# First conditioning vectors on TensorE in four column quarters, x first in the queue, and the first three projections cut in two along K

## The chip, the cores and the metric

The kernel runs on one core of one Trainium2 chip. The metric is device time of one execution in microseconds (us). Three runs of the kernel before took 1870.29, 1872.89 and 1874.12 us; the median, 1872.89, is what the change is held against. The profile comes from a further execution, which took 1885.09 us.

The names used below: PE is TensorE (matrix products; "PEld" its weight loads), DVE is VectorE, ACT is ScalarE, POOL is GpSimd, SP is the engine whose queue issues nearly all DMAs.

## The reference

Two layers over x (512 tokens by 1024 features), conditioned by a vector c. Layer 0 runs a state-space mixer (SSD) and a dilated window attention side by side; layer 1 is a convolution module; each layer ends with a SwiGLU FFN. What matters here is how the first layer begins:

```python
cs = jax.nn.silu(c)
for i in range(DEPTH):
    mod = cs @ ada_w[i] + ada_b[i]                       # 1024 -> 6*1024
    sh1, sc1, g1, sh2, sc2, g2 = [m[:, None, :] for m in jnp.split(mod, N_MOD, axis=-1)]
    h = rms_norm(x, norm_mix_g[i]) * (1 + sc1) + sh1
    ...
    z, xbc, dt_raw, q, k, v = jnp.split(h @ w_in, HY_SPLITS, axis=-1)   # hybrid_mixer
    xbc = jax.nn.silu(causal_depthwise_conv(xbc, conv_w, conv_b))
    xs, bm, cm = jnp.split(xbc, (SSM_D_INNER, SSM_D_INNER + SSM_GROUPS * SSM_STATE), axis=-1)
    dt = jax.nn.softplus((dt_raw + dt_bias).astype(jnp.float32))
    y = ssd_chunked(xs, dt, A, bm, cm)
```

Before any product with `w_in` can start, h needs the row statistics of x, the scale sc1 and the shift sh1, and these two are a vector-matrix product with 8 MB of `ada_w`.

## The kernel before

Activations are held transposed: feature tiles of 128 partitions by 512 tokens, eight of them (`h[k]`, k = 0..7). An exact product in float32 is made of three fast ones: weight and activation are each split in a high part and a low remainder (`hi`, `lo`; `hh`, `hl`), and `products` adds hi·hh, lo·hh and hi·hl over the eight k into one PSUM bank (24 matmuls of 128x512 for 128 output features).

The conditioning vectors are made in pieces of 512 columns, called by their first 128-column block: slabs 8 and 12 hold the scale (features 0-511 and 512-1023), slabs 0 and 4 the shift. Each slab is two DMAs of 1 MB (`ada_load`, `adaw`). `ada_wide` works on DVE: `adaa` = sum over k of `adaw[k]` times the scalar `cs[k]`, eight DVE operations of 128x512 (L160, L162); then `ada_finish` turns the result with four PE transposes (`ada`, L153) and sums over the free axis (`mod`, L155), adds the bias (L156). From slab 8 and 12 comes the gain `g_mix0`.

x is loaded as four token blocks `xin`. ACT squares them with a running sum (L316), a short DVE chain makes the reciprocal root (`rsqrt`), ACT scales the blocks (`xn`, L320), PE turns them (`xnp`, L331), ACT multiplies by the gain (`n_g`, L338), adds the shift and rounds to the high part (`n_h`, L341), DVE makes the low part (`n_l`, L343). x itself is turned too (`xtp`) and kept as `xT` (copied by ACT, L346).

The weight slabs of the projections (`slab`) are loaded by SP, rounded by ACT (`_h`, L194), and the remainder is made by the engine given (`_l`, L195): POOL for the first four slabs (`SL`), DVE after. The order of the first projections is dt (`wdt`), B and C of group 0 (`wbc0`, banks `bc0_0` and `bc0_1`), then four tiles of x (`wx`), four of z (`wz`). Two PSUM banks of the tag `pj` take turns for them: a new product can start only when the bank before last has been read, by ACT and three convolution steps of DVE (`conv_tile`, L443, L446).

dt goes through a long chain of small DVE operations (L403 to L419), a cumulative sum on PE, and a round trip through DRAM (`a_dram`, back as `ar` and `ef`) before the chunk loop of group 0 (`ssm_group`) can run. While that loop runs, PE makes the products of group 1, and so on for four groups. POOL makes further conditioning vectors in between (`ada_pool`, `adap`).

The order of the instructions on each engine is set by the Tile framework's scheduler from the program order and its own costs; `tc.issue_after` holds instructions behind a named one (here all of `after_ada` behind the last `ada_w` load, the first products behind the last transposes of slab 4). Semaphores keep the data right, the order is fixed at build time.

Of the kernel before, what the change touches and what calls it, by code (L numbers as in the profile page):

```python
# [17 lines left out]
P = 128  # L18
T = 512
# [58 lines left out]
def trunk_kernel(ctx: ExitStack, tc, a, out, dbg=None):  # L78
# [54 lines left out]
    S.activation(cs, pc, AF.Silu)  # L133
    slabs = {8: ada_load(first, 0, 8, nc.sync, 6)}
    pa = rows([(r128(a["norm_mix_g"][0]), 8), (r128(a["norm_ffn_g"][0]), 8),
               (r128(a["ada_b"][0]), 48), (r128(a["hy_conv_b"][0]), 24), (r128(a["hy_ssm_norm_g"][0]), 16)], "pa")
    xin = [first.tile([P, D], F32, tag="xin", name=f"xin{b}", bufs=NB) for b in range(NB)]
    for b in range(NB):
        nc.sync.dma_start(xin[b], a["x"][0, b * P:(b + 1) * P, :])
# [18 lines left out]
    def ada_wide(pool, tag, l, j0, ws):  # L158
        acc = pool.tile([P, 512], F32, tag=tag, name=f"adaa{l}_{j0}")
        V.tensor_scalar(acc, ws[0][:, 0, :], cs[:, 0:1], None, op0=ALU.mult)  # L160
        for k in range(1, KT):
            V.scalar_tensor_tensor(acc, ws[k // 4][:, k % 4, :], cs[:, k:k + 1], acc, op0=ALU.mult, op1=ALU.add)  # L162
        return ada_finish(l, acc, j0, 4)

# [154 lines left out]
    for b in range(NB):  # L319
        S.mul(xn[b], xin[b], rs[:, b:b + 1])  # L320
    g_mix0 = const.tile([P, KT], F32, name="g_mix0")
    for j0 in (8, 12, 0, 4):
        last_ada = ada_wide(tmp, "st_sq", 0, j0, slabs[j0])
        if j0 >= 8:
            k = slice(j0 - 8, j0 - 4)
            V.scalar_tensor_tensor(g_mix0[:, k], mod[0][:, j0:j0 + 4], 1.0, nmg0[:, k], op0=ALU.add, op1=ALU.mult)

# [7 lines left out]
    h = []  # L335
    for k in range(KT):
        t = first.tile([P, T], F32, tag="xg", name=f"n0_g{k}", bufs=KT)
        S.mul(t, turned(xn, k, "A" if k % 2 else "B", "xnp"), g_mix0[:, k:k + 1])  # L338
        hh = hpool.tile([P, T], F32R, tag="hh", name=f"n0_h{k}")
        hl = hpool.tile([P, T], F32R, tag="hl", name=f"n0_l{k}")  # L340
        S.activation(hh, t, AF.Identity, bias=mod[0][:, k:k + 1])  # L341
        with tc.issue_after(last_ada.ins) if LATE else nullcontext():
            V.scalar_tensor_tensor(hl, t, mod[0][:, k:k + 1], hh.bitcast(F32), op0=ALU.add, op1=ALU.subtract)  # L343
        h.append((hh, hl))
    for k in range(KT):
        S.copy(xT[k], turned(xin, k, XTP[k % 2], "xtp"))  # L346
    ctx_f.close()

    if "h" in dbg:
        for k in range(KT):  # L350
            t = tmp.tile([P, T], F32, tag="st_sq", name=f"dbgh{k}")
            V.tensor_tensor(t, h[k][0].bitcast(F32), h[k][1].bitcast(F32), op=ALU.add)
            nc.sync.dma_start(dbg["h"][k * P:(k + 1) * P, :], t)


    win = a["hy_w_in"][0]
    after_ada = tc.issue_after(marks["ada"].ins) if AFT else nullcontext()
    after_ada.__enter__()
# [16 lines left out]
    nc.sync.dma_start(nega, a["hy_a_log"][0:1, :].broadcast_to([P, HEADS]))  # L375

# [7 lines left out]
    w = slab([(win[:, 5120:5248], KT, P)], "wdt", SL[0])  # L384
    after_ada.__exit__(None, None, None)
    with tc.issue_after(marks["adat"].ins) if GDT else nullcontext():
        (dps,) = products(w, [grid(P, 0)], h, "dt")
# [65 lines left out]
    def ssm_inputs(g):  # L453
        w = slab([(win[:, 4096 + g * P:4096 + (g + 1) * P], KT, P), (win[:, 4608 + g * P:4608 + (g + 1) * P], KT, P)],
                 f"wbc{g}", SL[1] if g == 0 else V)
        pb, pc = products(w, [grid(P, 0), lambda k: 1024 + k * P], h, f"bc{g}")
# [3 lines left out]
        for j in range(2):  # L460
            o = 2048 + g * 512 + j * 256
            w = slab([(win[:, o:o + 256], KT, 256)], f"wx{g}_{j}", SL[2 + j] if g == 0 else V)
# [630 lines left out]
```

## Time and profile before

| What | us |
|---|---|
| median of three runs | 1872.89 (1870.29 to 1874.12) |
| profiled execution, whole | 1885.09 |
| its span, first to last instruction | 1882.8 |
| PE busy in the span | 1774.7 (94%) |
| DVE / ACT / POOL busy | 1046.5 / 693.1 / 430.5 |
| chain of work that ended last: PE, DVE, DMA | 73%, 11%, 7% of the span |

The profiled execution is 12 us longer than the median, so differences are worked out inside the profile and then set against the median. PE counts as busy from a matmul's start to its modelled end; two fast matmuls of 128x512 in a row start 0.23 us apart at full clock although each is recorded with 0.39 us. A float32 matmul appears as two records.

### The profile page before, as it was taken

The page shows a single profiled execution, that of the slowest core. Times are in us where ns is not written, and L with a number is a line of the kernel's source. Part 1 is how long each engine was busy: PE and PEld are TensorE (multiplying, and loading weights), DVE is VectorE, ACT ScalarE, POOL GpSimd, SP SyncE. Part 2 cuts the span into 40 slices and gives each one's busy share as a digit, 9 for nine tenths or more (in the row PEclk, how much of TensorE's full clock was granted, in tenths as well). Part 3 has the DMA queues.
Part 4 walks back from the last instruction along what each step waited for, and adds up shares of the span by engine and source line. Part 5 has one row for each costly group of instructions (what it writes and reads, how often), then busy time and mean ns, then how long its engine had stood idle before and what let it go on. Part 6 is the DMA issues. An engine that isn't in the chain of part 4 may idle for free.

```text
span 1882.8 us, 24868 instructions
## 1 busy us (share of the span) xinstructions
PE 1774.7 (94%) x9735; PEld 1450.0 (77%) x9735; DVE 1046.5 (56%) x1978; ACT 693.1 (37%) x1331; POOL 430.5 (23%) x328
## 2 busy tenths in 40 slices
PE   5897978999999999997999999999999999999998
PEld 3676766777778878777888888897567988888888
DVE  7858687755565565558665664373204743333336
ACT  6333333334545454344421221253214632122225
POOL 1437686422443440003000000013020200000001
PEclk8998989999999999997999999999998999999999
DMA  8354454545444443424555553253640523322223
GB/s 301 102 138 140 141 141 134 137 112 152 123 128 149 133 125 122 124 74 141 181 190 190 188 201 114 79 169 80 180 132 1 169 77 102 101 89 93 87 94 130
DMA packets 232066, 247.84 MB, mean 132 GB/s; under 512 B 13946, under 2 KB 198076, under 8 KB 231949
## 3 DMA queue, kind: packets, MB, share of 16 engines
q1 hardware_dynamic: 220813, 204.31, 36.6%
q0 software_dynamic: 11136, 41.95, 6.8%
q8 instruction: 77, 1.26, 0.3%
q14 instruction: 40, 0.33, 0.1%
HBM read 228.73 MB, written 8.64 MB: 126 GB/s over the span
## 4 chain that ended last, share of the span: by engine, by line
PE 73%; DVE 11%; DMA 7%; ACT 3%; issue 2%; POOL 2%; SPq 1%; DVEq 0%; ACTq 0%; POOLq 0%
PE fd L207 4%; PE fd L208 4%; PE fd L210 4%; PE fg L208 4%; PE fg L207 4%; PE fu L207 4%; PE fu L208 4%; PE fu L210 4%; PE fg L210 4%; PE cps L959 2%; PE s L717 2%; DMA ar<-a_dram 2%; PE wa L207 1%; PE wa L208 1%; PE wa L210 1%
## 5 line engine op out<-in xcount | busy, mean ns | idle before, releaser
L249 POOL TENSOR_TENSOR n_acc<-n_acc,n_q 128x256 f32<-128x256 f32 x32 | 29.7, 929 | 561.8 <-ACT n_q L245 561.7
L207 PE MATMUL fd<-uh,wd_h 128*128 128x512 f32 (+1 forms) x448 | 148.6, 347 | 0.9 <-DVE xT L592 0.9
L195 DVE TENSOR_TENSOR wf_l<-wf_w,wf_h 128x1024 fp32r<-128x1024 f32 x88 | 106.1, 1241 | 74.4 <-ACT wf_h L194 74.4
L208 PE MATMUL fd<-uh,wd_l 128*128 128x512 f32 (+1 forms) x448 | 147.0, 344 | 0.0
L194 ACT CAST wf_h<-wf_w 128x1024 fp32r<-128x1024 f32 x88 | 87.7, 1048 | 115.7 <-PE fd L210 71.9
L208 PE MATMUL fg<-n_h,wf_l 128*128 128x512 f32 x320 | 126.1, 394 | 2.0 <-DVE wf_l L195 2.0
L207 PE MATMUL fg<-n_h,wf_h 128*128 128x512 f32 x320 | 126.3, 395 | 0.7 <-ACT wf_h L194 0.5
L208 PE MATMUL fu<-n_h,wf_l 128*128 128x512 f32 x320 | 124.7, 390 | 0.0
L207 PE MATMUL fu<-n_h,wf_h 128*128 128x512 f32 x320 | 124.6, 389 | 0.0
L172 POOL TENSOR_TENSOR adap<-adap 128x128 f32<-128x128 f32 (+2 forms) x96 | 103.5, 1082 | 4.7
L869 DVE TENSOR_TENSOR fs<-fs,fu 128x512 f32<-128x512 f32 x40 | 27.5, 688 | 130.2 <-PE fu L210 130.2
L743 ACT ACTIVATE s<-s,nm 128x128 f32<-128x128 f32 x192 | 79.4, 415 | 50.7 <-DVE nm L739 40.4
L194 ACT CAST wd_h<-wd_w 128x1024 fp32r<-128x1024 f32 (+1 forms) x64 | 57.1, 941 | 101.2 <-PE fd L210 80.6
L592 DVE SCALAR_TENSOR_TENSOR xT<-fd,mod,xT 128x512 f32<-128x512 f32 (+1 forms) x64 | 39.1, 615 | 98.1 <-PE fd L210 97.8
L207 PEld LDWEIGHTS fd<-uh,wd_h 128*128 128x128 f32 x448 | 84.1, 188 | 12.0 <-DVE xT L592 1.3
L208 PEld LDWEIGHTS fd<-uh,wd_l 128*128 128x128 f32 x448 | 84.2, 188 | 10.5
L210 PE MATMUL fd<-ul,wd_h 128*128 128x512 f32 (+1 forms) x448 | 91.9, 343 | 0.0
L170 POOL TENSOR_TENSOR adap<-adap,cs 128x1024 f32<-128x1024 f32 x32 | 67.6, 2112 | 90.3 <-DMA adap<-in_ada_w 90.2
L195 DVE TENSOR_TENSOR wd_l<-wd_w,wd_h 128x1024 fp32r<-128x1024 f32 (+1 forms) x64 | 67.7, 1090 | 34.7 <-ACT wd_h L194 34.4
L162 DVE SCALAR_TENSOR_TENSOR adaa<-adaw,cs,adaa 128x512 f32<-128x512 f32 x112 | 84.8, 758 | 2.6
L210 PEld LDWEIGHTS fd<-ul,wd_h 128*128 128x128 f32 x448 | 72.9, 188 | 10.6
L210 PE MATMUL fg<-n_l,wf_h 128*128 128x512 f32 x320 | 79.1, 389 | 0.0
(400 smaller groups left out, 4584.5 us busy)
## 6 DMA issues: line engine op xcount, KB each, us to landing
adaw<-in_ada_w POOLq DMA_DIRECT2D x24, 1024.0 KB, 5.7
wf_w<-in_ffn_w_gate SPq DMA_DIRECT2D x22, 1024.0 KB, 5.2
wf_w<-in_ffn_w_up SPq DMA_DIRECT2D x22, 1024.0 KB
adap<-in_ada_w POOLq DMA_DIRECT2D x32, 512.0 KB, 5.5
wd_w<-in_ffn_w_down SPq DMA_DIRECT2D x16, 1024.0 KB, 5.1
wd_w<-in_ffn_w_down SPq DMA_DIRECT2D x16, 768.0 KB, 4.6
wa_w<-in_hy_w_out SPq DMA_DIRECT2D x20, 512.0 KB, 4.1
u<-cu SPq DMA_DIRECT2D x128, 67.5 KB, 2.0
```

The source lines that it names most:

```text
L162: V.scalar_tensor_tensor(acc, ws[k // 4][:, k % 4, :], cs[:, k:k + 1], acc, op0=ALU.mult, op1=ALU.add)
L170: G.tensor_tensor(w3, w3, cs.unsqueeze(2).broadcast_to([P, KT, P]), op=ALU.mult)
L172: G.tensor_tensor(w[:, 0:n], w[:, 0:n], w[:, n:2 * n], op=ALU.add)
L194: S.copy(hi[:, s:e], raw[:, s:e])
L195: eng.tensor_tensor(lo[:, s:e], raw[:, s:e], hi[:, s:e].bitcast(F32), op=ALU.subtract)
L207: PE.matmul(ps[:, cols], hi[:, o(k):o(k) + P], xh, start=k == 0, stop=False)
L208: PE.matmul(ps[:, cols], lo[:, o(k):o(k) + P], xh, start=False, stop=False)
L210: PE.matmul(ps[:, cols], hi[:, o(k):o(k) + P], acts[k][1][:, cols], start=False, stop=k == nk - 1)
L592: V.scalar_tensor_tensor(xT[m][:, cols], ps[:, cols], mod[l][:, go + m:go + m + 1], xT[m][:, cols], op0=ALU.mult, op1=ALU.add)
L717: marks[hp, 0] = marks[hp, 1] = PE.matmul(ps[:, o:o + 2 * wd].rearrange("p (e w) -> p e w", e=2), q, k, start=True, stop=True)
L743: S.activation(s[:, o:o + wd], s[:, o:o + wd], AF.Exp, bias=nm, accum_out=l)
L959: PE.matmul(ps[g * 32:(g + 1) * 32, :], w4[k][:, g * 8 + m, :], u4[k][:, g, t:t + w], start=m == 0, stop=m == 7)
```

## The change

1. SP's queue: x (four blocks) is issued ahead of slab 8; after that come the dt weights, slab 0, the B and C weights, slab 12 and slab 4. The loads of `wx0_0` and `wx0_1` are held behind the last `ada_w` load.
2. The four vectors are made by `ada_rows` on PE: silu(c) lies in column 0 of a 32-column weight tile (`cs32`, the other 31 columns zero); for each k a float32 matmul of 128 rows by 32 columns with 512 moving columns goes to one quarter of the output partitions (quarter k mod 4), so a vector takes eight such matmuls (`adar`). DVE copies the bank (`adas`), four float32 matmuls with one column of ones add the partitions (`adac`), one DVE operation adds the bias. The 32 DVE operations of 128x512, the 16 transposes and the 4 reductions of before are gone.
3. Two of the four `xn` blocks are scaled by DVE instead of ACT, and `xT` is copied by DVE instead of ACT.
4. The remainders of `wdt`, `wbc0`, `wx0_0`, `wx0_1` are made by DVE instead of POOL.
5. h is made in two halves of features (k = 0..3, k = 4..7). The products of dt, B and C are made for the first half, then for the second (`first_products`), and a fixed order is written out between them: dt and B first half; slab 12; C first half; slab 4; dt, B and C second half. C takes a bank of tag A instead of `pj`.

```diff
+    xin = [...]                                   # now ahead of slab 8
+    for b in range(NB):
+        nc.sync.dma_start(xin[b], a["x"][0, b * P:(b + 1) * P, :])
+    cs32 = first.tile([P, KT, 32], F32, name="cs32", bufs=1)
+    V.memset(cs32, 0.0)
+    V.tensor_copy(cs32[:, :, 0], cs)
     slabs = {8: ada_load(first, 0, 8, nc.sync, 6)}
...
-    slabs[12] = ada_load(first, 0, 12, nc.sync, 6)
-    for j0 in (0, 4):
-        slabs[j0] = ada_load(first, 0, j0, nc.sync, 6)
...
+    def ada_rows(l, j0, ws):
+        ps = bank("C", f"adar{l}_{j0}")
+        for k in range(KT):
+            g = k % 4
+            PE.matmul(ps[g * 32:(g + 1) * 32, :], cs32[:, k, :], ws[k // 4][:, g, :], start=k < 4, stop=k >= 4)
+        rw = tmp.tile([P, 512], F32, tag="st_sq", name=f"adas{l}_{j0}")
+        V.tensor_copy(rw, ps)
+        pm = bank("C", f"adac{l}_{j0}", (P, 4))
+        for j in range(4):
+            marks['adac', j0] = PE.matmul(pm[:, j:j + 1], rw[:, j * P:(j + 1) * P], ones[:, 0:1], start=True, stop=True)
+        marks['mod', j0] = V.tensor_tensor(mod[l][:, j0:j0 + 4], pm, adab[l][:, j0:j0 + 4], op=ALU.add)
...
-        S.mul(xn[b], xin[b], rs[:, b:b + 1])
+        if b % 2:
+            marks['xn'] = V.tensor_scalar(xn[b], xin[b], rs[:, b:b + 1], None, op0=ALU.mult)
+        else:
+            S.mul(xn[b], xin[b], rs[:, b:b + 1])
...
-    for j0 in (8, 12, 0, 4):
-        last_ada = ada_wide(tmp, "st_sq", 0, j0, slabs[j0])
...
+    def first_gain(j0):
+        ada_rows(0, 8 + j0, slabs[8 + j0])
+        kk = slice(j0, j0 + 4)
+        V.scalar_tensor_tensor(g_mix0[:, kk], mod[0][:, 8 + j0:12 + j0], 1.0, nmg0[:, kk], op0=ALU.add, op1=ALU.mult)
+        for k in range(j0, j0 + 4):
+            t = ng[k] = first.tile([P, T], F32, tag="xg", name=f"n0_g{k}", bufs=6)
+            S.mul(t, turned(xn, k, "BABABABB"[k], "xnp"), g_mix0[:, k:k + 1])
+
+    def first_shift(j0):
+        ada_rows(0, j0, slabs[j0])
+        for k in range(j0, j0 + 4):
+            hh, hl = h[k]
+            S.activation(hh, ng[k], AF.Identity, bias=mod[0][:, k:k + 1])
+            V.scalar_tensor_tensor(hl, ng[k], mod[0][:, k:k + 1], hh.bitcast(F32), op0=ALU.add, op1=ALU.subtract)
...
+    first_gain(0)
+    wdt = slab([(win[:, 5120:5248], KT, P)], "wdt")
+    slabs[0] = ada_load(first, 0, 0, nc.sync, 6)
+    wbc0 = slab([(win[:, 4096:4096 + P], KT, P), (win[:, 4608:4608 + P], KT, P)], "wbc0")
...
+    for j0 in (12, 4):
+        slabs[j0] = ada_load(first, 0, j0, nc.sync, 6)
+    with after('xn'):
+        for k in range(KT):
+            V.tensor_copy(xT[k], turned(xin, k, XTP[k % 2], "xtp"))
+    first_shift(0)
+    pre = [(wdt, grid(P, 0), bank("pj", "dt_0")), (wbc0, grid(P, 0), bank("pj", "bc0_0")),
+           (wbc0, lambda k: 1024 + k * P, bank("A", "bc0_1"))]
+
+    def first_products(jobs, ks):
+        for (hi, lo), o, ps in jobs:
+            for k in ks:
+                PE.matmul(ps, hi[:, o(k):o(k) + P], h[k][0], start=k == 0, stop=False)
+                PE.matmul(ps, lo[:, o(k):o(k) + P], h[k][0], start=False, stop=False)
+            for k in ks:
+                marks['fp'] = PE.matmul(ps, hi[:, o(k):o(k) + P], h[k][1], start=False, stop=k == KT - 1)
+
+    first_products(pre[:2], range(0, 4))
+    with after('fp'):
+        first_gain(4)
+    with after(('adac', 12)):
+        first_products(pre[2:], range(0, 4))
+    with after('fp'):
+        first_shift(4)
+    with after(('adac', 4)):
+        first_products(pre, range(4, KT))
...
+            with after('ada') if g == 0 else nullcontext():
+                w = slab([(win[:, o:o + 256], KT, 256)], f"wx{g}_{j}")
```

Three places in the order of instructions matter below. Names carry the layer or group first and a buffer number last: `adar0_12` is layer 0, slab 12; `n0_h4` is the high part of feature tile 4.

On PE, between the first products and their end. Before, dt and B run through all eight feature tiles:

```order
L153 MATMUL ada0_4_209<-cst_72,adaa0_4_200 128x128 x4
L110 MATMUL cw_p_363<-cst_72,cw_r_361 128x96
L207 MATMUL dt_0_399<-n0_h0_231,wdt_h_393 128x512
L208 MATMUL dt_0_399<-n0_h0_231,wdt_l_394 128x512
L207 MATMUL dt_0_399<-n0_h1_242,wdt_h_393 128x512
L208 MATMUL dt_0_399<-n0_h1_242,wdt_l_394 128x512
```

Now, after the last first-half product of B:

```order
L407 MATMUL bc0_0_336<-n0_l3_156,wbc0_h_226 128x512
L170 MATMUL adar0_12_362<-adaw0_12_0_254,cs32_95 32x512 x4
L170 MATMUL adar0_12_362<-adaw0_12_1_256,cs32_95 32x512 x4
L341 MATMUL xnp4_381<-cst_72,xn0_114 128x128
...
L175 MATMUL adac0_12_373<-ones_74,adas0_12_371 128x1 x4
L404 MATMUL bc0_1_337<-n0_h0_149,wbc0_h_226 128x512
...
L170 MATMUL adar0_4_420<-adaw0_4_0_258,cs32_95 32x512 x4
L170 MATMUL adar0_4_420<-adaw0_4_1_260,cs32_95 32x512 x4
...
L175 MATMUL adac0_4_431<-ones_74,adas0_4_429 128x1 x4
L404 MATMUL dt_0_335<-n0_h4_157,wdt_h_213 128x512
```

Slab 12, sixteen transposes of `xn` and slab 4 now stand in PE's queue between the two halves of the products; before, all of them stood ahead of the first product.

On DVE, ahead of the first shift. Before, the low parts of h follow the last bias add at once:

```order
L113 COPY cw_365<-cw_p_363 128x96
L156 TENSOR_TENSOR mod0_121<-mod0_121,pa_99 128x4
L343 SCALAR_TENSOR_TENSOR n0_l0_232<-n0_g0_224,mod0_121,n0_h0_231 128x512
L343 SCALAR_TENSOR_TENSOR n0_l1_243<-n0_g1_235,mod0_121,n0_h1_242 128x512
L343 SCALAR_TENSOR_TENSOR n0_l2_254<-n0_g2_246,mod0_121,n0_h2_253 128x512
```

Now:

```order
L208 TENSOR_TENSOR wbc0_l_227<-wbc0_w_223,wbc0_h_226 128x1024
L378 TENSOR_SCALAR cwh_238<-cw_236 128x96
L208 TENSOR_TENSOR wbc0_l_227<-wbc0_w_223,wbc0_h_226 128x1024
L465 TENSOR_SCALAR nega_251<-nega_251 128x32
L172 COPY adas0_0_319<-adar0_0_310 128x512
L176 TENSOR_TENSOR mod0_112<-adac0_0_321,pa_110 128x4
L368 SCALAR_TENSOR_TENSOR n0_l0_150<-n0_g0_183,mod0_112,n0_h0_149 128x512
```

The copy that closes slab 0 stands behind the remainder of the B and C weights and behind `nega`, both of which wait for ACT.

On SP, the DRAM round trip of dt's cumulative sum. Before:

```order
L435 DMA a_dram_384<-arow_471 32x512
L186 DMA wbc1_w_1110<-in_hy_w_in 128x8x128 x2
L486 DMA ar0_0_844<-a_dram_384 128x8x128
L561 DMA b_dram_826<-bv_832 16x896
L486 DMA ar0_1_880<-a_dram_384 128x8x128
L186 DMA wx1_0_w_1185<-in_hy_w_in 128x8x256
L186 DMA wx1_1_w_1259<-in_hy_w_in 128x8x256
```

Now:

```order
L199 DMA wbc1_w_1117<-in_hy_w_in 128x8x128 x2
L199 DMA wx1_0_w_1192<-in_hy_w_in 128x8x256
L483 DMA a_dram_483<-arow_537 32x512
L199 DMA wx1_1_w_1266<-in_hy_w_in 128x8x256
L538 DMA ar0_0_851<-a_dram_483 128x8x128
L613 DMA b_dram_833<-bv_839 16x896
L565 DMA ef0_1_914<-a_dram_483 64x4x128 x2
L538 DMA ar0_1_887<-a_dram_483 128x8x128
```

The first read of `ar` moved behind both x weight loads of group 1, the second also behind the first `ef` loads.

More of the change, by code (lines that the diff above doesn't have):

```diff
@@ L334, in trunk_kernel @@
     xT = [const.tile([P, T], F32, name=f"xT{k}") for k in range(KT)]
[L335 to L353, printed above, removed]
+    h = [(hpool.tile([P, T], F32R, tag="hh", name=f"n0_h{k}"), hpool.tile([P, T], F32R, tag="hl", name=f"n0_l{k}"))
+         for k in range(KT)]
```

36 lines of the change are left out of this document (20 added, 16 removed).

## The prediction

> **What bounds the kernel now.** I read the stretches of the span first (columns: PE, PE weight loads, DVE, ACT, POOL busy us, then the granted TensorE clock, DMA share, GB/s), then the DMA rate in slices of 3.25 us from the start.
>
> ```profile
> 0.00:40.00 40.00, 17.71 (x86) 12.96 (x87) 28.93 (x60) 26.20 (x40) 4.27 (x7) 0.90 0.91 310
> 60.00:70.00 10.00, 4.80 (x20) 3.30 (x18) 9.96 (x8) 0.84 (x1) 10.00 (x7) 1.00 0.34 105
> 70.00:80.00 10.00, 7.52 (x28) 6.18 (x29) 8.07 (x14) 2.41 (x5) 3.14 (x4) 0.83 0.34 107
> 80.00:130.00 50.00, 49.32 (x250) 38.41 (x248) 28.31 (x38) 19.83 (x28) 10.22 (x6) 1.00 0.49 131
> 130.00:180.00 50.00, 38.38 (x186) 29.93 (x187) 44.73 (x54) 18.50 (x28) 35.18 (x23) 0.89 0.41 117
> 400.00:1882.00 1482.00, 1439.22 (x8098) 1188.07 (x8096) 751.60 (x1592) 540.59 (x1109) 221.03 (x177) 0.98 0.41 126
> ```
>
> ```profile
> GB/s 61 367 378 400 391 388 387 386 388 311 293 66 44 332 294 72 282 6 3 0 239 83 163 160 5 0 72 271 0 137 84 159 284 5 0 269 198 123 117 297
> ```
>
> From 400 us on PE is busy 97% of the time, so what the start wins or loses is carried to the end. PE stands idle 22.3 us in the first 40, 7.7 from 60 to 80, 11.6 from 130 to 180 (there DVE is busy 44.7 of 50). DMA runs at some 388 GB/s until 35.75 us: eleven slices, 12.2 MB, which is ada_w, x, and the dt, B and C weights.
>
> The chain of waits (start, us) and the rows in time order say what opens the products and what stalls later:
>
> ```profile
> 2.06 7.62 DMA adaw<-in_ada_w
> ...
> 36.08 1.67 DVE adaa L162
> 37.79 1.11 PE ada L153 x4
> ...
> 38.77 0.78 PE L207 MATMUL dt<-n_h,wdt_h 128*128 128x512 f32 x1
> ...
> 50.09 0.57 ACT L389 COPY draw<-dt 32x512 f32<-32x512 f32 x1 [6.21 <-PE dt L210]
> ...
> 56.16 1.98 PE L210 MATMUL bc<-n_l,wbc_h 128*128 128x512 f32 x8
> ...
> 64.46 0.50 PE L208 MATMUL x<-n_h,wx_l 128*128 128x512 f32 x1 [3.34 <-POOL wx_l L195]
> ...
> 72.48 0.47 PE L207 MATMUL x<-n_h,wx_h 128*128 128x512 f32 x1 [4.34 <-DVE sc L446]
> ...
> 80.29 0.78 ACT L443 ACTIVATE sx<-x,cbh,cwh 128x512 f32<-128x512 f32 x1 [0.48 <-PE x L210]
> ```
>
> The last slab's DVE sums end at 37.8; products start at 38.8; dt is read at 50.1; C ends at 58.1; the second x tile ends at 80.3, after stalls of 3.3 us (POOL late with a remainder) and 4.3 us (a bank not yet read).
>
> **The change part by part.**
>
> *Transfers.* Same bytes, other order. x takes slab 8's place and lands at 2.06 + 7.62 = 9.7 instead of 15.1 (last square below). At 2.7 us for 1.05 MB the rest lands: slab 8 at 15.1, dt weights 16.5, slab 0 21.9, B and C 24.6, slab 12 30, slab 4 35.6, x weights 38 and 41. SP's queue now holds slab 12 behind slab 0's landing, with 1 MB of B and C still queued (2.7 us): 0 to 1 us of gap, I take 0; nothing waits for it, since PE comes to slab 12 later.
>
> ```profile
> 15.14 1.06 ACT L316 ACTIVATE xn<-xin 128x1024 f32<-128x1024 f32 x1
> 16.33 0.17 DVE L317 TENSOR_SCALAR n_ss<-n_ss 128x4 f32<-128x4 f32 x1 [0.28 <-ACT xn L316]
> ...
> 20.62 0.15 DVE L226 SCALAR_TENSOR_TENSOR n_y<-n_t,n_y 128x4 f32<-128x4 f32 x1
> 21.10 4.27 ACT L320 ACTIVATE xn<-xin,n_y 128x1024 f32<-128x1024 f32 x4
> ...
> 116.71 1.09 PE L504 MATMUL pd<-ar,xdt 128*64 128x128 f32 x16
> 117.73 1.12 PE L526 MATMUL pst<-xde,btok 128*128 128x512 f32 x2
> 118.69 0.39 PE L497 MATMUL pb<-sc,sb 128*128 128x128 f32 x2
> 118.91 0.60 PE L492 MATMUL px<-cst,sx 128*128 128x128 f32 x4
> ```
>
> *Norm.* The squares end at 11.0. The DVE chain of 12 small steps takes 4.4 us between rows of `adaa`; free of them, at 0.2 us a step, 2.4: 13.4. Two blocks on ACT, two on DVE: `xn` ready at 15.5 instead of 25.4.
>
> *One vector on PE.* No row has quarter-width matmuls. A float32 128x512 starts its follower 0.96 us later (`pst`, 117.73 to 118.69). One after another, eight cost 7.7 us; four abreast, 1.9. The nearest row is `pd`: eight of half width, alternating halves, take 1.02 us, where eight of full width cost 8 x 0.22 (`pb` to `px`) = 1.76, so halves overlap to 0.58. Twice that step, 0.58 squared times 7.7, gives 2.6; I take 2.4, near the abreast end because of `pd`. The Trainium skill, "TensorEngine Tiling (Array Packing)", Tiling Modes, has 128x32 as four independent tiles but says that a change of tiling mode drains the array; by its full fourfold the vector would cost 1.9 and the sum below gain 1.5 us more. The `pd` row agrees in kind; no run here shows quarters.
>
> ```profile
> 14.96 0.69 DVE L155 TENSOR_REDUCE mod<-ada 128x4 f32<-128x512 f32 x1 [1.21 <-PE ada L153]
> ...
> 26.21 4.74 ACT L338 ACTIVATE n_g<-xnp,g_mix 128x512 f32<-128x512 f32 x8
> 26.96 2.39 PE L331 MATMUL xnp<-cst,xn 128*128 128x128 f32 x16 [0.89 <-ACT n_g L338]
> 30.97 1.28 ACT L416 ACT_TABLE_LOAD   x1
> 32.77 2.56 ACT L341 ACTIVATE n_h<-n_g,mod 128x512 fp32r<-128x512 f32 x4
> 36.27 2.17 ACT L194 CAST wbc_h<-wbc_w 128x1024 fp32r<-128x1024 f32 x2
> ...
> 95.43 1.20 DVE L195 TENSOR_TENSOR wz_l<-wz_w,wz_h 128x1024 fp32r<-128x1024 f32 x1
> ```
>
> *First products.* Slab 8 on PE from 17 (behind eight transposes and `pa`), partly at half clock, 3 us; copy 0.7 (as L155's read of a bank), column sums 0.6, two adds: gain at 24. ACT: four `n_g` at 0.59 to 26.5, B and C casts 2.17, table load and `nega` 1.5: 30.3. On DVE the copy for slab 0 stands behind the B and C remainders (2 x 1.2) and `nega`: 30.5 to 31.2, though slab 0 itself left PE before 30. Sums, bias, first `n_h` 0.64: first product at 33.1, 5.7 earlier. The eight `xT` copies, 0.7 each, lie on DVE before that, beside the wait for slab 8.
>
> *To the end of C.* PE now has in its queue: 72 products at 0.227 ((1.98 - 0.39)/7) = 16.3; slabs 12 and 4, 4.8; 16 transposes, 2.4; eight column sums, 1.2; waits for copy, bias and `n_h` after each slab, 2.4. Together 27.1: C ends at 60.2, 2 us later than before, and dt with it, 10 us later. The early start is eaten by what moved between the halves.
>
> *The x tiles.* Their high parts queue on ACT behind the read of dt (60 to 62), the remainders on DVE, not on a busy POOL: tile 0 runs 62 to 67.5. Tile 1 waits for B's bank: four remainders (4.8) and five convolution steps (0.67 each) on DVE from 61.4 to 70, plus 2 for POOL's `adap`, which still runs then. It ends at 78, 2 us ahead of before: from C's end to there two tiles of 5.45 us lose 7 us now, 11.3 before (22.2 less 10.9), where the two stalls were followed by a stretch at half clock (0.83 in the row from 70).
>
> ```profile
> 52.49 0.29 DVE L403 TENSOR_TENSOR dt_v<-dt_t,dtb 128x128 f32<-128x128 f32 x1 [0.90 <-PE dt_t L392]
> 56.72 2.36 DVE L410 TENSOR_TENSOR dt_w<-dt_w 128x128 f32<-128x128 f32 x1
> 74.45 0.29 DVE L419 TENSOR_TENSOR dta<-dt_v,nega 128x128 f32<-128x128 f32 x1
> 98.91 0.36 SPq L486 DMA_DIRECT2D ar<-a_dram  x1
> 105.30 1.90 POOL L487 TENSOR_TENSOR ar<-ar,acs 128x1024 f32<-128x1024 f32 x1 [4.51 <-DMA ar<-a_dram]
> 147.29 0.47 PE L207 MATMUL x<-n_h,wx_h 128*128 128x512 f32 x1 [2.89 <-DVE sc L446]
> ```
>
> *Group 0's loop.* dt's chain ran slowly beside POOL (2.36 us against 0.29 for one size). It starts 10 us later now but without that, ending near 85 (74.7 before). Six more tiles bring PE to 112; B and C of group 1 (11 us) now stand ahead of the first `pd`, so PE needs it at 123.5 and tile 1 of group 1 can start at 136, against 147.3: a lead of 11.3. But DVE then still owes what it had done before by that place: one `xdt`, two `ar` minima, one `ar` product, three `y` steps, 0.7 each and 1.2: 5.3. From 130 to 180 DVE sets the pace, so 6 us are left, and later groups repeat the same work. The norm of layer 1's FFN is finished one tile later: 0 to 2.8 us, covered by other products, 0.
>
> Sum: -6 against the profiled 1885.09; against the median of 1872.89, 1867.
>
> **Rivals.** (a) *Quarters run in turn.* 7.7 us each: 5.3 more in each of slabs 0, 12, 4, 16 in all; part of it, 6, hides in the stalls. -6 + 16 = +10: 1883. For it: no quarter row. Against: `pd`.
> (b) *The loop of group 0 comes too late*, the other side again. Issue to POOL takes 6.4 us (98.91 to 105.30), then 1.9, 0.7, 1.1, 1.2: 11.3 from `ar`'s issue to `pd`. The second `ar` is queued behind `b_dram`, which needs the last `bv` product after the z tiles: issue at 113.5, ready 125, wanted about 126. Slack 1 us. If the dt chain is slowed beside POOL as before (12 us), 11 of it stall PE: -6 + 12 = +6, 1879. It decides from 6 us of lateness on.
> (c) *No change.* PE works in bits from 14 to 33, so its clock stays at half: slabs 8 and 0 each 2.4 longer, first products late by as much: 4.5 lost, -1.5, 1871. For it: four transposes took 1.11 us at 37.79 after an idle 6.6, but 0.6 each time in the sixteen at 26.96. The Trainium skill, "TensorE: Matmul & The Clock Gate", Part 1, asks a busy window of 3.4 us before full clock; by that rule this case is the likely one early on, and the 0.90 of the first stretch neither bears it out nor excludes it. I keep it below the forecast because of the sixteen.
> (d) *More is kept.* DVE's idle 22 us between 80 and 130 take up what it owes, and the stalls to 180 shrink: -15, 1858.
>
> **Chances.** Forecast 0.40 (1861 to 1869); (d) 0.17; (c) 0.21; (a) 0.08; (b) 0.14. A change of 0.2%, 3.7 us, is about what a measurement can tell: faster 0.57, same 0.21, slower 0.22. The range, 1851 to 1881, takes in all but the far ends of (a), (b) and (d).
>
> **What would show it.** Right: last square at 11, slab in 2 to 3 us, first product near 33, C's end near 60, tile 1 of group 1 near 136. A slab at over 5 us is (a); PE waiting for DVE `ar` at the first `pd` of group 0 is (b); product starts 0.43 us apart beyond 37 is (c). Wrong altogether if C ends before 55 or after 65.

## The result, and the profile after

After took 1893.53 us (median of four runs, 1887.70 to 1898.47), before 1871.72 us (four runs, 1870.29 to 1874.12): 1.0108 times before, 95% interval 1.0081 to 1.0134. A second comparison (e5) gave 1.0085 (1.0063 to 1.0107). The forecast was 1867 us, 6 us faster; it is some 16 to 22 us slower.

The first profile of before was a long one: a further execution of it took 1874.67 us with a span of 1872.5, and 9.7 of the 10.3 us between the two spans lie behind the end of the SSM groups at 414 us. So after is read here against that further profile. The stretches of after (columns as in the prediction):

```profile
0.00:40.00 40.00, 24.56 (x129) 15.51 (x133) 18.38 (x45) 17.79 (x26) 0.19 (x4) 0.96 0.98 330
60.00:70.00 10.00, 5.96 (x17) 4.46 (x18) 9.62 (x8) 4.98 (x7) 10.00 (x7) 0.68 0.22 59
70.00:80.00 10.00, 9.56 (x41) 7.59 (x41) 9.53 (x20) 2.94 (x5) 1.36 (x2) 0.98 0.53 164
80.00:130.00 50.00, 48.86 (x222) 38.04 (x221) 26.51 (x42) 17.68 (x26) 8.36 (x5) 1.00 0.42 116
130.00:180.00 50.00, 36.27 (x204) 28.21 (x204) 46.03 (x49) 15.26 (x21) 27.44 (x19) 0.89 0.41 113
180.00:400.00 220.00, 188.02 (x940) 146.96 (x941) 170.13 (x192) 77.87 (x113) 147.18 (x106) 0.93 0.51 139
400.00:1891.00 1491.00, 1447.99 (x8158) 1194.20 (x8156) 757.36 (x1601) 545.30 (x1115) 224.92 (x179) 0.98 0.41 126
```

and two of the further execution of before:

```profile
130.00:180.00 50.00, 37.37 (x183) 29.21 (x184) 43.88 (x52) 18.90 (x28) 33.93 (x22) 0.89 0.41 110
180.00:400.00 220.00, 198.35 (x998) 155.83 (x997) 156.64 (x192) 76.76 (x112) 137.32 (x102) 0.94 0.51 142
```

In the first 40 us PE does 6.9 us more than in the first profile of before, as meant. But from 180 to 400 us PE does 10.3 us less than in the further one, and DVE is busy 13.5 us longer for the same number of instructions (192). About half of the loss, 8 to 9 us, stands at the end of the SSM groups, far behind the lines that were changed; the rest lies behind them. DVE's longer time is not what costs: a version further down without the loss (e13) has it too, 171.46 us.

The first stage, rows in time order on PE and ACT of after:

```profile
16.38 3.29 PE L170 MATMUL adar<-adaw,cs 128*32 128x512 f32 x16
...
26.91 1.92 PE L170 MATMUL adar<-adaw,cs 128*32 128x512 f32 x16
...
32.34 0.50 PE L404 MATMUL dt<-n_h,wdt_h 128*128 128x512 f32 x1 [1.07 <-ACT n_h L367]
...
39.32 0.39 PE L407 MATMUL bc<-n_l,wbc_h 128*128 128x512 f32 x1
39.64 1.92 PE L170 MATMUL adar<-adaw,cs 128*32 128x512 f32 x16
41.50 1.53 PE L341 MATMUL xnp<-cst,xn 128*128 128x128 f32 x12
...
58.88 1.07 PE L407 MATMUL bc<-n_l,wbc_h 128*128 128x512 f32 x4
```

```profile
59.08 0.58 ACT L437 COPY draw<-dt 32x512 f32<-32x512 f32 x1 [5.82 <-PE dt L407]
...
79.10 0.78 ACT L491 ACTIVATE sx<-x,cbh,cwh 128x512 f32<-128x512 f32 x1 [0.81 <-PE x L223]
```

A vector takes 1.92 us on PE, the first product starts at 32.3 us, dt is read at 59.1, C ends at 60.0, the second x tile at 79.1. Up to here the change does what was forecast.

What PE waited for between 60 and 425 us (total us, times, longest), in the further execution of before and in after:

```profile
PE z L207 <- DVE sx L446: 12.1, 2, 9.0
PE pb L520 <- DVE cb L499: 5.6, 1, 5.6
PE x L207 <- DVE sc L446: 5.1, 3, 2.9
...
PE pd L504 <- DVE ar L500: 1.3, 1, 1.3
```

```profile
PE pb L572 <- DVE cb L551: 12.6, 2, 12.2
PE x L220 <- DVE sc L494: 9.2, 2, 6.6
PE z L220 <- DVE sx L494: 7.7, 1, 7.7
PE pd L556 <- DVE ar L552: 5.8, 4, 4.0
PE x L221 <- DVE wx_l L208: 3.7, 1, 3.7
```

Longer in after are the waits of `pd` for `ar`, 5.8 us in all and 4.0 at once, where before has 1.3, and those for `cb` and `sc`. Where the first comes from stands in SP's queue and on PE, in the further execution of before and then in after:

```profile
84.70 0.33 SPq L435 DMA_DIRECT2D a_dram<-arow  x1
...
93.60 0.37 SPq L486 DMA_DIRECT2D ar<-a_dram  x1
```

```profile
92.54 1.03 PE L559 MATMUL bv<-hot,tab 33*16 33x256 f32 x4
...
116.47 1.09 PE L504 MATMUL pd<-ar,xdt 128*64 128x128 f32 x16
```

```profile
97.44 0.33 SPq L483 DMA_DIRECT2D a_dram<-arow  x1
107.38 0.37 SPq L199 DMA_DIRECT2D wx_w<-in_hy_w_in  x1
115.60 0.37 SPq L538 DMA_DIRECT2D ar<-a_dram  x1
```

```profile
114.97 0.60 PE L611 MATMUL bv<-hot,tab 33*16 33x256 f32 x2
...
132.90 1.98 PE L556 MATMUL pd<-ar,xdt 128*64 128x128 f32 x16 [4.04 <-DVE ar L552]
```

`hot` and `bv` are two small tables of the attention's bias, which three small products make while group 0's z tiles run. They are allocated under the tag `ar`, in the same two buffers as the `ar` of the chunk loop. So the first `ar` can be loaded only when the last `bv` product has read `hot`, and in after the scheduler put that product behind the z tiles: it ends at 115.6 us and the load follows 0.03 us later, 18 us after the write to `a_dram`. The buffer accounts for the last eight of these 18 us: for the first ten the load stands in SP's queue behind `wx1_1`, a weight load of group 1, which is issued at 107.4. In the further execution of before the last `bv` products start at 92.5 and the load stands at 93.6, 9 us after the write. Loop 0's first `pd` then comes at 132.9 us instead of 116.5; of these 16 us PE spends 4.0 waiting, the rest with B and C of group 1, which now stand ahead of it, and with the other work of its order.

The group ends, read from the four stores to `yd_dram`, show how that goes on. All kernels of the study (each ratio against before on the same chip; ten runs of each, four of after and of e14; before ran 13 or 25 times beside them):

| Kernel | median us | times before (95%) | groups end at, us |
|---|---|---|---|
| before, second profile | 1874.67 (one run) | | 179, 271, 364, 414 |
| after (e5) | 1893.76 | 1.0085 (1.0063 to 1.0107) | 179, 276, 378, 421 |
| e2 after, low parts on POOL | 1886.54 | 1.0044 (1.0022 to 1.0067) | 185, 277, 367, 416 |
| e3 before, low parts on DVE | 1874.02 | 0.9977 (0.9950 to 1.0004) | 176, 268, 359, 407 |
| e4 first products whole | 1877.20 | 1.0005 (0.9986 to 1.0024) | 170, 282, 380, 416 |
| e6 one low part on POOL, before's order | 1879.99 | 1.0016 (1.0001 to 1.0031) | 184, 277, 370, 419 |
| e7 e4 in before's order | 1873.21 | 0.9987 (0.9968 to 1.0006) | 179, 271, 365, 414 |
| e8 cut along K, order left free | 1880.41 | 1.0023 (1.0010 to 1.0036) | 169, 270, 371, 417 |
| e9 after, POOL quiet | 1879.20 | 1.0033 (1.0007 to 1.0059) | 172, 268, 370, 414 |
| e10 e3, POOL quiet | 1863.03 | 0.9945 (0.9915 to 0.9975) | 171, 264, 352, 401 |
| e11 e7, POOL quiet | 1861.29 | 0.9939 (0.9911 to 0.9967) | 170, 267, 353, 400 |
| e12 e9, early `ar` | 1868.75 | 0.9957 (0.9937 to 0.9977) | 171, 265, 359, 403 |
| e13 after, early `ar` | 1873.43 | 0.9989 (0.9977 to 1.0001) | 176, 270, 365, 409 |
| e14 e11, early `ar` | 1859.45 | 0.9925 (0.9896 to 0.9954) | 163, 256, 346, 395 |

### The profile page after: what moved, and what is told of

It is laid out like the page before. It is cut to its first block, busy times and chain, and to the rows that moved or that the text cites. A ratio compares the mean times of both kernels' runs of the same rounds, so it can differ in the third digit from the quotient of the medians.

```text
span 1891.6 us, 24992 instructions
## 1 busy us (share of the span) xinstructions
PE 1779.9 (94%) x9815; PEld 1448.2 (77%) x9815; DVE 1044.2 (55%) x1966; ACT 687.8 (36%) x1321; POOL 421.5 (22%) x320
## 4 chain that ended last, share of the span: by engine, by line
PE 75%; DVE 11%; DMA 6%; ACT 3%; issue 2%; POOL 2%; SPq 1%; DVEq 0%; ACTq 0%; POOLq 0%
PE fd L220 4%; PE fd L221 4%; PE fd L223 4%; PE fg L221 4%; PE fu L221 4%; PE fu L220 4%; PE fu L223 4%; PE fg L223 4%; PE fg L220 4%; PE cps L1011 3%; PE s L769 2%; DMA ar<-a_dram 1%; PE qq L220 1%; PE qq L221 1%; PE qq L223 1%
## 5 line engine op out<-in xcount | busy, mean ns | idle before, releaser
L185 POOL TENSOR_TENSOR adap<-adap 128x512 f32<-128x512 f32 (+2 forms) x96 | 110.2, 1156 | 4.0
L221 PEld LDWEIGHTS fd<-uh,wd_l 128*128 128x128 f32 x448 | 84.2, 188 | 10.5
L223 PEld LDWEIGHTS fd<-ul,wd_h 128*128 128x128 f32 x448 | 72.9, 188 | 10.6
L223 PE MATMUL fu<-n_l,wf_h 128*128 128x512 f32 x320 | 79.0, 389 | 0.0
## 6 DMA issues: line engine op xcount, KB each, us to landing
u<-cu SPq DMA_DIRECT2D x128, 67.5 KB, 2.0
```

What stands on the lines that cost most here:

```text
L185: G.tensor_tensor(w[:, 0:n], w[:, 0:n], w[:, n:2 * n], op=ALU.add)
L221: PE.matmul(ps[:, cols], lo[:, o(k):o(k) + P], xh, start=False, stop=False)
L223: PE.matmul(ps[:, cols], hi[:, o(k):o(k) + P], acts[k][1][:, cols], start=False, stop=k == nk - 1)
```

## The experiments

Three causes were weighed at first: dt comes nine us later ("late dt"); the low parts (remainders) of the first slabs moved from POOL to DVE; and the order that the scheduler lays in the groups, whatever the data times. Later a fourth came up: the late first load of `ar`.

**e1 and e5: both kernels once more.** No edit.

> The kernel before, word for word, for one more profile. Its first profiled execution took 1885.09 us, 13 us more than the median of its other runs, so that only 8.8 of the 21.8 us of the result stand in the two traces compared so far. If that execution was the odd one, this one takes 1869 to 1876 us, and its trace shows some 13 us less in one stage. If every profiled execution of this kernel is slow, it takes some 1885 us again and the stage stays hidden. Either way dt's product ends at 50 us and the last group of the SSM is stored at 403 to 415 us.

> The kernel after, word for word, beside before on the same chip, with one more profile. If the result holds it takes 1.0108 times before, 1890 to 1897 us where before takes some 1872 to 1876, and the last group is stored at 423 us again, the four groups ending 97, 101 and 44 us apart; what its trace loses beyond 423 us tells how much of the 21.8 us lies behind the groups. If the first comparison was partly chance, the ratio falls to 1.005.

Before took 1874.67 us, so its first profile was a long one. After held: 1.0085. In e5's trace the group ends come 97, 102 and 43 us apart and the last is 7.5 us later than before's; the last transposes of the program start 13.4 us later (1877.5 against 1864.0). So about half of the difference stands in the groups of these two traces. The rest lies behind them, where before alone varied by 9.7 us between its two profiles, and no run explains it.

**e2 and e3: the low parts.** In e2 the seven subtractions of after go back to POOL, in e3 before gets them on DVE:

```diff
 # e2, on after
-    wdt = slab([...], "wdt")                        # and wbc0, wx0_0, wx0_1
+    wdt = slab([...], "wdt", G)
 # e3, on before
-    SL = (G, G, G, G)
+    SL = (V, V, V, V)
```

> After with one part undone: the low parts of wdt, wbc0 and both halves of wx of group 0 are made on POOL again and not on DVE (seven subtractions, some 8.4 us of DVE between 15 and 67 us). Everything else of the change stays, dt's product still ends at 59 us or a little later. Theory 'low parts': these subtractions on DVE, and the order that the planner lays behind them, cost the time; then this kernel goes back to 1866 to 1876 us, with the first load of ar right behind a_dram's store. Theory 'late dt': the nine us by which dt ends later cost it, through the loop of group 0; then it stays at 1886 to 1896 us. Theory 'any order': the groups come out by some 10 us differently with each small edit; then it may be anywhere from 1870 to 1895 us, and dt's and the low parts' times won't go with it.

> Before with that part alone: the low parts of wdt, wbc0 and wx of group 0 on DVE instead of POOL; dt's product stays where it was, around 50 us or some us later because DVE is busy with the vectors until 45 us. Theory 'low parts': slower by 10 to 20 us (1882 to 1892). Theory 'late dt': no more than the 3 to 5 us by which dt comes later, 1872 to 1877 us. Theory 'any order': anywhere from 1865 to 1895.

e3 isn't slower, 0.9977, so the low parts on DVE cost nothing by themselves. e2 came halfway, 1.0044: 1886.5 us is just inside what "late dt" and "any order" had given it and far above what "low parts" had. From the first `pd` of group 0 on, e2's rows on PE stand in exactly before's order, and so do e3's; after's don't. With before's order the groups are 230 to 235 us long from the first end to the last (e2 231, e3 231, before 235), with after's 242. In e2 and e3, as in before, the first `ar` is also loaded early, at 99 and 95 us, so these two runs don't tell the order from the load. e2 pays for it ahead of the groups: PE waits 4.9 us for a low part on POOL, and group 0 ends 6 us later.

**e4 and e8: the cut along K and its written-out order.** e4 multiplies dt, B and C whole; e8 keeps the cut but takes out the four `after(...)` around it.

```diff
-    first_products(pre[:2], range(0, 4))
-    with after('fp'):
-        first_gain(4)
-    with after(('adac', 12)):
-        first_products(pre[2:], range(0, 4))
-    with after('fp'):
-        first_shift(4)
-    with after(('adac', 4)):
-        first_products(pre, range(4, KT))
+    first_gain(4)                                   # e4
+    first_shift(4)
+    first_products(pre, range(0, KT))
```

> After without the two parts along K: dt, B and C are multiplied whole, in that order, when all of h is there (some 51 us); the rest of the change stays. PE then stands idle or at half clock until 51 us, dt ends at some 57 us (24 matmuls of 0.23 to 0.43 us), C at 69 us, 9 us later than now. Theory 'late dt': dt 2 us earlier, C 9 us later, so 1893 to 1903 us. Theory 'low parts': the first products hardly matter, 1890 to 1900 us. Theory 'any order': anywhere from 1870 to 1900. If it is faster than after by more than 5 us, the split itself was the loss.

> After without the written-out order: the cut along K stays in the program, the waits between the halves, slab 12 and slab 4 are taken out, so that the planner may place them. It puts slabs 12 and 4 ahead of most of the products, as in the whole-K run, and gives the groups a third order that is neither before's nor after's. Theory 'the written-out order is late': dt ends at 53 to 55 us, some 5 earlier than in after, and the time is 1875 to 1884 us. Theory 'order in the groups': the first stage gains those 5 us, but a third order loses in the groups as the two others did, the group ends 242 us or more from the first to the last (before 235), 1877 to 1892 us.

Whole products were 15 us faster than after (1.0005 against 1.0085), where "late dt" and "low parts" had both expected a loss. Left alone in e4, the scheduler still starts dt, B and C on the first four k, lays slabs 12 and 4 between them and ends dt at 53 us and C at 57.5, 6 and 2.5 us earlier than the written-out order does. It had been expected that PE would stand idle until 51 us; it doesn't. The lead is then lost: e4's group 0 ends 9 us ahead of before, its last group 2 us behind; e8, whose dt ends at 56 us, likewise (169 and 417, 248 us from the first end to the last). Each has its own order in the groups. What looked like the price of the split goes in e13, further down, although the split stays.

**e6 and e7: before's order in the groups.** One choice of engine is enough to bring it back:

```diff
 # e6, on after; e7, on e4, with j == 1
-                w = slab([(win[:, o:o + 256], KT, 256)], f"wx{g}_{j}")
+                w = slab([(win[:, o:o + 256], KT, 256)], f"wx{g}_{j}", G if g == 0 and j == 0 else V)
```

> After with one thing different: the low part of the first x slab of group 0 (two subtractions of 128x1024) is made on POOL as before. That is 2.4 us of DVE, but the planner now lays PE's instructions from the first pd of group 0 to the end of the groups in just the order of before; first stage and dt's end (59 us) stay as in after. Theory 'order': the loss of the groups comes from the order, not from late data; then the groups end 92, 92 and 50 us apart as in before, the last at 411 to 416 us, and the kernel takes 1874 to 1882 us, 11 to 18 less than after. Theory 'late dt': the loop of group 0 still starts late and the last group ends at 420 us or later, 1888 to 1896 us.

> The first products whole, not cut along K (as in the run before, 1877 us), and the low part of the second x slab on POOL: by that the planner keeps before's order in the groups to the last row. The first stage ends as in the whole-K run: dt 53 us, C 57, last z tile of group 0 at 108 us instead of 117. Theory 'order': the lead of some 8 us at the end of group 0 stays to the last group, which is stored at 403 to 408 us (before 414), 1864 to 1870 us where before takes 1874 to 1876. Theory 'late dt' or 'the loops bound the groups': the lead is lost by the second group as it was in the whole-K run, 1874 to 1879 us.

e6 takes back 13 us of after's loss, 0.7% of the time. dt still ends at 60 us, yet `ar` is loaded at 98 us and the first `pd` runs at 120: of the ten us by which dt is late only four reach the loop's load (94 us in before), so "late dt" falls. But `ar` now comes 18 us earlier than in after, together with before's order, and e6 doesn't tell the two apart. The last store came at 419 us and not at 411 to 416, because PE waited 7.3 us for the low part that now lies on POOL. e7 kept its group lengths too (92, 94, 49) but not the lead: its last z tile of group 0 ended at 115 us, not 108, so it tied with before.

**e9, e10 and e11: POOL quiet behind the first products.** POOL makes two conditioning vectors (`adap`) between 60 and 71 us. They now read a copy of silu(c) that DVE makes behind `dta`:

```diff
     V.tensor_tensor(by_head(dta), ...)
+    cs2 = const.tile([P, KT], F32, name="cs2")
+    V.tensor_copy(cs2, cs)                          # kept behind dta on DVE
...
-        G.tensor_tensor(w3, w3, cs.unsqueeze(2)...)
+        G.tensor_tensor(w3, w3, cs2.unsqueeze(2)...)
```

> After with POOL kept quiet in the stretch behind the first products: the two conditioning vectors that POOL makes there (adap, 60 to 71 us) read a copy of silu(c) that DVE makes only when dt's chain has reached dta, so they run from some 85 us on. One DVE copy of 128x8 is added; the order on PE, DVE and SP from the first pd to the end of the groups is that of after, row for row. In after DVE's two low parts of the first x slab took 2.56 us each beside POOL, 1.2 elsewhere. Both theories: x's first tile starts its low products 3 us earlier, the stall of 3.7 us is gone, the last z tile of group 0 ends at 111 to 113 us instead of 115. Theory 'order': the groups are still 97, 101 and 44 us apart, so the last is stored at 418 to 421 us, 1888 to 1892 us, 1.005 to 1.009 times before. Theory 'lateness' (the groups lose because loop 0's data come late): most of the loss goes with the 3 to 5 us, 1876 to 1884 us.

> Before with the low parts of the first four slabs on DVE (as in the third run of this study) and POOL quiet until dta in the same way; before's order in the groups. DVE's low parts of x take 1.2 us each and not 2.56, dt's chain ends some 4 us earlier. Theory 'order': in this order a lead of the first stage is kept to the end: group ends some 3 us ahead of that run's 176, 268, 359 and 407, 1866 to 1871 us, 0.994 to 0.997 times before. Theory 'the groups are bound by themselves' (a lead is never kept): 1872 to 1876 us as without it.

> The kernel with whole first products and before's order in the groups (1873 us) and POOL quiet until dta, but for the low part of the second x slab. Theory 'order': the first x tile's low parts at 1.2 instead of 2.4 us and dt's steps of 2.4 us back at 0.3 bring the last z tile of group 0 to 108 to 111 us and loop 0 some 3 to 5 us forward; the groups stay 92, 93 and 49 us apart, the last stored at 408 to 411 us, 1867 to 1871 us. Theory 'bound by themselves': 1872 to 1876 us. POOL's vectors now run beside z's tiles and may hold up the first ar by up to 4 us; then 1872 us too, with a wait of POOL's ar behind adap in the trace.

DVE's two low parts of x and POOL's two multiplies, first in after, then in e9:

```profile
61.89 5.12 DVE L208 TENSOR_TENSOR wx_l<-wx_w,wx_h 128x1024 fp32r<-128x1024 f32 x2
```

```profile
59.93 3.80 POOL L183 TENSOR_TENSOR adap<-adap,cs 128x1024 f32<-128x1024 f32 x2 [3.09 <-DMA adap<-in_ada_w]
```

```profile
60.07 2.35 DVE L208 TENSOR_TENSOR wx_l<-wx_w,wx_h 128x1024 fp32r<-128x1024 f32 x2
```

```profile
82.83 4.20 POOL L183 TENSOR_TENSOR adap<-adap,cs 128x1024 f32<-128x1024 f32 x2 [26.80 <-DVE cs L470]
```

5.12 us beside POOL, 2.35 without; PE's wait for the low part falls from 3.7 to 1.0 us. In e9 every row from the first `pd` to the end of the groups stands as in after, and the four groups end 7 to 8 us earlier than in e5: here a lead that comes in at group 0 is kept to the last group, with the order unchanged. By the ratios e9 gains 0.5%, about 10 us: the time lies where "lateness" had put it, while the groups keep the lengths that "order" had named (96, 102 and 44). e9 and e10 then start the groups level: POOL quiet and low parts of x on DVE in both, group 0 done at 172 and 171 us. The last group is stored at 414 us in after's order and at 401 in before's, 1.0033 against 0.9945 times before. This too is order and load together: `ar` is loaded at 110 us in e9 and at 90 in e10. e10 and e11 came out below the times that either theory had given them (1863 and 1861 us, e11's last group at 400 us and not at 408 to 411; e10's ratio is as "order" had it). Both beat both kernels. The quiet POOL is no part of what was changed and can be had in before too: from e3 to e10 the ratios give 6 us, which is within their two intervals.

**e12, e13 and e14: an early first `ar`.** The tables leave the two buffers of `ar` for that of `y1`, which isn't needed before the first `pd`:

```diff
-    hot = ssm.tile([P, HPG, P], F32, tag="ar", name="hot")...[0:33, 0:LTOT]
+    hb = ssm.tile([P, 4, T], F32, tag="y1", name="hb", bufs=1).rearrange("p h l -> p (h l)")
+    hot = hb[0:33, 0:LTOT]
...
-    bv = ssm.tile([P, HPG, P], F32, tag="ar", name="bv")...[0:16, 0:LTOT]
+    bv = hb[0:16, LTOT:2 * LTOT]
```

> After with POOL quiet (the ninth run, 1879 us), and the tables hot and bv put into the buffer of y1 instead of the two buffers of ar: there the first load of ar waited until the last bv product, which the planner had put behind the z tiles (ar's load at 110 us, the first pd at 128 after a stall of 4.1 us). Now the load can follow a_dram's store, some 8 us earlier; the planner also moves some rows of the groups (146 on DVE, 246 on PE), far fewer than lie between after's order and before's. Theory 'late ar' (that stall and what follows from it make the groups 242 us long instead of 230): the stall goes, the groups come to 92 to 96 us apart, the last stored at 402 to 406 us, 1865 to 1871 us. Theory 'order' (loop 0's work lies behind B and C of group 1 on PE, and the stalls of 5, 13 and 8 us later come from the order itself): the long stalls of the later groups stay, 240 us or more from the first group's end to the last, 1874 to 1881 us.

> After with one edit: the tables hot and bv lie in the buffer of y1 and not in the two buffers of ar, so that the first load of ar need not wait for the last bv product (115 us). POOL is as in after. Theory 'late ar': ar's load comes at 99 to 105 us instead of 115.6, the first pd without its stall of 4.0 us, the groups are 230 to 235 us long from the first one's end to the last one's instead of 242, and the kernel takes 0.997 to 1.003 times before, some 8 to 14 us less than after. Theory 'order beyond it': 1.006 times or more, the groups still 240 us long.

> The fastest version so far (whole first products, before's order in the groups, POOL quiet, 0.9939) with the same edit. Its first load of ar stood at 89.6 us, 0.4 behind the last bv product; PE's order in the groups doesn't change. Theory 'late ar': nothing to win, since PE comes to the first pd only at 107 us; 0.992 to 0.996, the last group stored at 399 to 402 us. If it gains 5 us or more, the two buffers of ar were a limit by themselves and not only in after's order.

e13 is after with this one edit, and it takes the whole loss back: 0.9989, 18 us less than after by the two ratios (1.0085 less 0.9989, intervals of 0.0022 and 0.0012). SP's queue and PE in e13:

```profile
99.04 0.33 SPq L483 DMA_DIRECT2D a_dram<-arow  x1
102.54 0.99 SPq L538 DMA_DIRECT2D ar<-a_dram  x2
113.63 0.37 SPq L199 DMA_DIRECT2D wx_w<-in_hy_w_in  x1
```

```profile
116.57 0.60 PE L612 MATMUL bv<-hb,tab 33*16 33x256 f32 x2
...
122.81 1.09 PE L556 MATMUL pd<-ar,xdt 128*64 128x128 f32 x16
```

The `bv` product still stands behind the z tiles, at 116.6 us, but both loads of `ar` are issued at 102.5, now ahead of `wx1_1` in the queue, and `pd` runs ten us earlier, ahead of C of group 1 on PE and without a stall. The same stretches as above:

```profile
80.00:130.00 50.00, 50.00 (x239) 39.15 (x239) 34.19 (x51) 20.43 (x30) 9.86 (x5) 1.00 0.45 124
130.00:180.00 50.00, 40.16 (x205) 31.13 (x205) 44.14 (x51) 20.54 (x29) 34.78 (x23) 0.88 0.44 122
180.00:400.00 220.00, 196.42 (x1020) 153.54 (x1019) 171.46 (x192) 75.91 (x110) 143.65 (x102) 0.96 0.53 141
```

PE gets 1.1, 3.9 and 8.4 us of work back in the three stretches, 13.4 together; DVE does 7.7 us more between 80 and 130, where it has room, and 1.9 less from 130 to 180, where it hasn't. e12 says the same with POOL quiet: 403 us for the last store instead of 414, so 11 of the 13 us between e9 and e10 go with this edit. The groups are 232 us long in both, as the theory "late ar" had it, though e13's longest stall (`pb` for `cb`, 12.3 us) is as long as in after. That stall wasn't the loss.

e14, where PE's order is before's and `ar`'s load already came early enough, gives 0.9925 against e11's 0.9939, no difference that these intervals can tell: no cost of the shared buffers shows where the last `bv` product is early. Its trace ends group 0 7 us and the last group 5 us ahead of e11; its dt had ended 2 us earlier already. It is the fastest version of the study, 14 to 16 us under before.

Three things stay open. The edit of e12 and e13 also lets the scheduler move rows of the groups (146 on DVE and 246 on PE, as the expectation of e12 says) and puts `ar` ahead of `wx1_1` in SP's queue, so that the freed buffers are shown to take the loss back, but the earlier data and the order that comes with them aren't separated. A late load alone needn't cost as much: e4 loads its first `ar` at 109 us, with B and C of group 1 ahead of `pd` as in after, and ties with before; and e8 loads `ar` at 98 us and still loses 2 to 7 us. What costs in these orders of their own wasn't tried. And e13 stores the last group 5 us ahead of before's further execution but ties with it by the runs: what the traces show behind the groups, 1450 to 1460 us from the last store to the last transposes, differs as much between the two executions of before as between any two kernels.

## Why the prediction was wrong

*Right in its marks, in part by luck: transfers, norm, vectors, first products, to the end of C.* Forecast and measured: last square 11.0 and 10.5; gain and first product 33.1 and 32.3; a vector 2.4 us and 1.92; C's end 60.2 and 60.0; dt 10 us later and 9.0; second x tile 78 and 79.1. Rival (a), quarters in turn at 7.7 us, is out: eight ran in 1.92 us, the lower bound. Its own sum, 16 us with 6 of them hidden, would have been 1877 and not 1883. Rival (c) is out for most of the way: products start 0.23 us apart from 36.3 us on, and of the vectors only the first ran partly at half clock (3.29 us). But the first ten products start mostly 0.43 us apart, as (c) has it, which costs 1.7 us that the sum didn't have; a first product 0.8 us early and two vectors 0.5 us shorter each set it off, and so C's end agrees to 0.2 us.

*Mis-sized, and set off: the low parts beside POOL.* The x tiles had four remainders at 1.2 us "plus 2 for POOL's `adap`"; the first two took 5.12 us instead of 2.35. PE waited 3.7 us and ran at half clock until 70 us, its products 0.43 us apart, so the first tile ended at 72.9 us, not 67.5. The second ended near its forecast only because it had been booked with a wait until 72 us, most of which then fell away. By e9 the slow low parts cost 7 to 10 us at the end of group 0. But before pays nearly as much for its own low parts on POOL, 3.4 us of stall and group 0's end at 179 us, so the difference between the two kernels is small here.

*The step that failed: "Group 0's loop".* It let PE need the first `pd` at 123.5 us, booked a lead of 11.3 us for B and C of group 1 standing ahead of it, took off 5.3 for DVE and closed with "6 us are left, and later groups repeat the same work". The lead didn't come: z ended at 115 us, where 112 was forecast and before has 117, and tile 1 of group 1 started at 146.0 us, not 136 (before 147.3). `pd` came at 132.9, 9 us after the forecast, and PE waited 4.0 us for it. And the later groups didn't repeat: group 0 ends within some 2 us of before's, the last group 7 to 9 us behind it. The groups took 242 us from the first end to the last, before 235; with the tables out of `ar`'s buffers (e13) they took 232.

*The rival that came nearest: (b), the loop of group 0 comes too late.* It named the place, the wait for the last `bv` product behind the z tiles, and gave it 0.14 and 1879 us. It looked at the second `ar` in the queue behind `b_dram` and found 1 us of slack. The first `ar` has none: it needs `hot`'s buffer, which a list of tags shows and a queue order doesn't. Its size was wrong as well: it had 12 us of stall at `pd`, where the stall itself took 4.0 us, and 1879 us, where 1893.53 were measured. By e13 the shared buffers, with all that the scheduler makes of them, cost 18 us. Without them the change takes as long as before, which is the time that (c) had, for another reason.

*The norm of layer 1's FFN*, 0 to 2.8 us, taken at 0: from the transpose `gf_p` to the last `f_a` product both traces of after take 64.4 to 64.5 us, both of before 62.9. Only after's two have a stretch of 3.4 us at half clock in it, which would make 1.7; e9, with after's order, lacks it and takes 63.0. So the term is 1.5 us in these traces, and not clearly the kernel's.

## What to carry to other kernels

When a scheduler sets the order, an early lead can be lost in the stage behind it: here it was kept where the order stayed the same (e9 against after) and lost in orders of their own (e4, e8). Compare the order of the stage that follows, and look there first for the loads that came later than their data. Before trusting a transfer's slack, list who else holds its buffers: a small table that shares a tag with a loop's tile makes the loop wait for whatever uses that table last. And keep GpSimd's elementwise work out of the stretch in which DVE is the pace-maker: here that was worth 6 to 10 us in three pairs of kernels, one of them (6) within its intervals; the change was forecast to win 6.

## What was not expected of the hardware

Four matmuls of a quarter's width run fully abreast: in after's trace the four of vector 12 start within 0.02 us of each other, and eight float32 ones of 128x512 took 1.92 us, 0.24 each, where one of full width starts its follower 0.96 us later. The switch there and back cost no more than 0.1 us: the row ahead of the quarters starts 0.32 us before them, where like rows start 0.23 apart, and the transposes behind start as the quarters end (39.32, 39.64, 41.50). The Trainium skill, "TensorEngine Tiling (Array Packing)", Tiling Modes, says that a change of mode drains the array; by these rows the drain is small.

Two DVE subtractions with both inputs in SBUF ran at less than half their speed beside POOL's multiplies and adds, 2.56 us against 1.2 each. The Trainium skill, "SBUF — State Buffer", SBUF: two separate sides, says that the two engines share one pair of ports, held for a whole instruction, so that the other waits. The trace agrees in kind: 2.8 us more for two subtractions, of which the first began beside the second of two multiplies of 1.9; POOL's adds followed.

Executions of one program differ more than was assumed: 25 runs of before on one chip lay between 1866.57 and 1884.60 us. Between its two profiles the part behind the groups differed by 9.7 us, and the clock records there show half clock for 47.8 and for 30.7 us, in both near 850 to 900 and 1430 to 1455 us, in the longer one also at 783 and 1527; half of the difference of 17.1 us is 8.5. Ten runs of a kernel here left an interval of 0.12 to 0.30% to either side, so a change of 0.2% can stay open even with ten.
